# Making the low halves of weight tiles with ACT and an adding transfer instead of DVE, in a fused attention, feed-forward and retention kernel

## The chip, the cores and the metric

The kernel runs on one core of a Trainium2 chip. The metric is device time in microseconds for one launch. The engines are named as the profile names them: PE multiplies matrices, DVE and ACT work on vectors, POOL and SP mostly issue transfers here.

## What is computed

Two transformer-like blocks in a row, on 512 tokens with 1024 channels, in fp32. The first is differential attention beside a gated convolution, then a feed-forward part with a short convolution; the second is two layers of retention beside a short convolution. Cut to the products with weights, which is where the work is:

```python
# first_block (528 positions: 16 meta tokens + 512)
z = rms(h) @ w_in                       # 1024 -> 7168: q, k, v, glu, two gates
u = glu_a * sigmoid(glu_b);  u = causal_dwconv(u, 31 taps);  u = silu(layernorm(u))
y_conv = u @ w_conv_out
m = sigmoid(g_att) * y_att + sigmoid(g_conv) * y_conv
h = h + m @ w_out
up = causal_dwconv(rms(h) @ w_up, 3 taps)   # 1024 -> 5632
h = h + (silu(gate) * val) @ w_down         # 2816 -> 1024
# second_block, two layers
proj = rms(x) @ w_in[l]                 # 1024 -> 8192: c_b, c_c, c_x, c_z, r_q, r_k, r_v, r_z
x = x + rms(concat(conv part, retention part) @ w_out[l])
```

## The kernel before

**How a product is made exact enough.** PE multiplies in a rounded fp32 format (`float32r`). To keep fp32 accuracy, each weight tile and each activation tile is held as two halves: a high half (the value rounded) and a low half (the value minus its high half). A product is then three passes: high weight by high activation, low weight by high activation, high weight by low activation. In `proj` (line 150) these are the three entries of `passes`; each pass is 8 matmuls over the 1024 rows, so one weight tile of 128 by 1024 feeds 24 matmuls per chunk of tokens.

**How weights come.** The list `order` holds all 300 weight tiles (512 KB each, eight of them 384 KB) in the order in which PE will use them. `prep` (line 126) brings the next one: SP issues the transfer of the raw tile into `wraw`, ACT writes the high half `wh` as a rounding copy (line 138), DVE writes the low half `wl` as raw minus high (line 139). `wraw` has two buffers; `wh` and `wl` have four each. `getw` (line 142) hands out tiles and keeps four prepared or in preparation, so the halves of tile i go into the buffers that tile i-4 leaves when PE is done with it. PE is done with `wl` after its second pass, and with `wh` after its third.

**What sets the order.** Each engine executes its own queue strictly in order; waits are on semaphores. The order within a queue is made at build time by a list scheduler that plays the program through a timeline of its own, so a changed instruction also moves others.

**The stages, in order of time.** Gated linear unit (PE tiles `gv`, `gg`), attention heads (`v`, `q`, `k`, `ga`, `gc`, with scores `s`, transposes `tr`, outputs `po`, and per-head sums `pss`), beside them the 31-tap convolution on DVE (line 405), then `yc` and `wo`, feed-forward `up` and `dn`, and twice a retention stage (`rv`, `rq`, `rk`, `rz`, `st`, `ro`), a convolution stage (`cc`, `cx`, `cb`, `cz`) and an output stage (`w`). The queue of POOL carries, before the change, the moves `qh` and `kk` of attention (eight per head, lines 493 and 506), `hre` (line 642), `dc` of retention (line 838) and a few additions.

Of the kernel before, what the change touches and what calls it, by code (L numbers as in the profile page):

```python
# [13 lines left out]
AF = mybir.ActivationFunctionType  # L14
ALU = mybir.AluOpType
# [25 lines left out]
KB = 1  # L41
PSF = (4, 3, 1)
GC_EARLY = 5

PAR = {}
_off = 0
# [17 lines left out]
def kernel(ctx, tc, hT, par, pos, decay, w1, w2, out):  # L64
    nc = tc.nc
    V, S, PE = nc.vector, nc.scalar, nc.tensor
# [7 lines left out]
    def fv(ap):  # L74
        return ap.bitcast(F32)
# [4 lines left out]
    def w1_tiles(name, idx):  # L80
        order.append((w1[name], idx))
# [4 lines left out]
    for h in range(HEADS):  # L86
# [5 lines left out]
        if h < HEADS - 1:  # L92
            w1_tiles("w_in", 40 + h)
        if h < GC_EARLY:
            w1_tiles("w_in", 48 + h)
    w1_tiles("w_in", 40 + HEADS - 1)
    for n in range(GC_EARLY, NK):
        w1_tiles("w_in", 48 + n)
# [27 lines left out]
    def prep():  # L126
        if state["next"] >= len(order):
            return
        src, idx = order[state["next"]]
        i = state["next"]  # L130
        state["next"] += 1
        src = src[idx]
        n = src.shape[1]
        raw = wpool.tile([P, D], F32, tag="wraw", bufs=2, name=f"wraw{i}")[:, :n]
        nc.sync.dma_start(raw, src)
        wl = wpool.tile([P, D], F32R, tag="wl", name=f"wl{i}")
        wh = wpool.tile([P, D], F32R, tag="wh", name=f"wh{i}")
        S.copy(wh[:, :n], raw)  # L138
        V.tensor_tensor(wl[:, :n], raw, fv(wh[:, :n]), ALU.subtract)  # L139
        ready.append((wh, wl))  # L140

    def getw():
        while len(ready) < LOOK + 1 and state["next"] < len(order):
            prep()
        return ready.pop(0)
# [37 lines left out]
    def later(steps, by=20000):  # L183

        at_ = tc.cur_priority
        tc.cur_priority = at_ + by
        steps()
        tc.cur_priority = at_
# [75 lines left out]
    for c0, cn in C528:  # L264
        for j in range(NK // 2):
            nc.sync.dma_start(ht2[j][:, :, c0:c0 + cn], hT[2 * j:2 * j + 2, :, c0:c0 + cn].rearrange("k p t -> p k t"))
            if c0 == 0 and j in (0, 3):
                prep()
        if c0 == 0:
            nc.sync.dma_start(pr[:, 8:], par[:, 8:])  # L270
# [167 lines left out]
    def g_conv(n):  # L438
        w = getw()
        if n < 6:  # L440
            t = ap1.tile([P, TQ], F32, name=f"tgc{n}")
        else:
            t = upool.tile([P, CONV_K - 1 + T1], F32, tag="u", name=f"tgc{n}")
        for i, (c0, cn) in enumerate(C514):
            ps = mmA(f"gc{n}_{i}")[:, :cn]
            proj(ps, w, xh, xl, TQ0 + c0, cn)
            S.activation(t[:, c0:c0 + cn], ps, AF.Tanh, scale=0.5)
        tgc.append(t)

    def g_att(h):  # L450
        w = getw()
        tg = ap2.tile([P, TQ], F32, tag="tga", name=f"tga{h}")
        for i, (c0, cn) in enumerate(C514):
            ps = mmA(f"ga{h}_{i}")[:, :cn]
            proj(ps, w, xh, xl, TQ0 + c0, cn)
            S.activation(tg[:, c0:c0 + cn], ps, AF.Tanh, scale=0.5)
        return tg
# [8 lines left out]
    for h in range(HEADS):  # L466
# [41 lines left out]
        if h < HEADS - 1:  # L508
            tg = g_att(h)
        if h < GC_EARLY:  # L510
            g_conv(h)
        if h == HEADS - 1:
            att_rstd(("kf", "kl"))
            tg = g_att(h)
            later(norm_2, N2)
            for n in range(GC_EARLY, NK):
                later(lambda: g_conv(n), GCL)
# [11 lines left out]
        for t, (q0, qn, nkey) in enumerate(QT):  # L529
# [40 lines left out]
            src = ptr[:, :nb * qw].rearrange("p (b q) -> p b q", b=nb)  # L570
# [190 lines left out]
    for l in range(2):  # L761
# [38 lines left out]
        for h in range(HEADS):  # L800
# [66 lines left out]
            for j, i0 in enumerate((0, 128, 256, 384)):  # L867
                n = SEQ - i0
# [203 lines left out]
```

## Time and profile before

| what | value |
|---|---|
| time, median of 3 runs | 1881.17 us (1880.52 to 1882.43) |
| the profiled execution: its own time | 1883.03 us |
| the profiled execution: span from first to last instruction | 1881.2 us |
| PE busy | 1852.5 us, 98% |
| DVE busy | 1311.3 us, 70% |
| ACT busy | 836.1 us, 44% |
| POOL busy | 76.6 us, 4% |
| transfers | 177.79 MB, mean 95 GB/s |
| mean granted clock of PE | 0.995 |

The profiled execution took 1.9 us more than the median, and 1.83 us of its time lie outside the span. A busy share is an average over stages; which engine holds up a stage is read from the waits of PE in it. A transfer that is in flight is not counted as busy time of the engine that issued it.

### The profile page before, as it was taken

How to read it: one execution, taken by the hardware profiler on the slowest of the kernel's cores; microseconds unless marked ns; L12 is line 12 of the kernel's file. 1: busy time of each engine (PE TensorE's matmuls, PEld its weight loads, DVE VectorE, ACT ScalarE, POOL GpSimd, SP SyncE). 2: the span in 40 equal slices, each digit the busy share in tenths (PEclk: the TensorE clock that was granted, in tenths of full speed). 3: DMA queues.
4: the chain of work that ended last, by engine and by line, in shares of the span. 5: the costliest groups of instructions: out<-in, count | busy, mean ns of one | idle time of the engine just before them, and what ended most of it. 6: DMA issues, size and time to landing. Idle time of an engine off the chain costs nothing.

```text
span 1881.2 us, 29256 instructions
## 1 busy us (share of the span) xinstructions
PE 1852.5 (98%) x11802; PEld 1685.7 (90%) x11802; DVE 1311.3 (70%) x2147; ACT 836.1 (44%) x1473; POOL 76.6 (4%) x123
## 2 busy tenths in 40 slices
PE   8999999999999999999999999999999999999997
PEld 7999999988999999988988888888899888888887
DVE  8999999876688777634588776454277877745424
ACT  7234455673445444433356553222355555422222
POOL 3000011000000000000000000000020000000000
PEclk9999999999999999999999999999999999999999
DMA  4332323222332222232323222222213222222221
GB/s 153 101 113 91 102 87 118 89 70 68 113 107 91 96 96 91 85 104 93 99 75 107 79 91 90 100 101 91 100 68 101 95 92 93 79 101 92 99 101 56
DMA packets 53047, 177.79 MB, mean 95 GB/s; under 512 B 6640, under 2 KB 10736, under 8 KB 52912
## 3 DMA queue, kind: packets, MB, share of 16 engines
q1 hardware_dynamic: 47696, 160.80, 24.8%
q0 software_dynamic: 5072, 15.12, 2.9%
q8 instruction: 93, 1.52, 0.3%
q14 instruction: 42, 0.34, 0.1%
q10 hardware_dynamic: 144, 0.00, 0.0%
HBM read 165.25 MB, written 2.10 MB: 89 GB/s over the span
## 4 chain that ended last, share of the span: by engine, by line
PE 96%; ACT 2%; DVE 1%; DMA 0%; issue 0%; POOL 0%; SPq 0%; DVEq 0%; ACTq 0%
PE up L157 13%; PE w L157 9%; PE dn L157 6%; PE rz L157 5%; PE cb L157 5%; PE cc L157 5%; PE cx L157 5%; PE cz L157 5%; PE rv L812 5%; PE rq L157 5%; PE rk L157 5%; PE v L479 3%; PE gc L157 3%; PE yc L157 3%; PE wo L157 2%; PE q L157 2%
## 5 line engine op out<-in xcount | busy, mean ns | idle before, releaser
L138 ACT CAST wh<-wraw 128x1024 fp32r<-128x1024 f32 (+1 forms) x300 | 313.3, 1045 | 490.3 <-PE dn L157 66.8
L139 DVE TENSOR_TENSOR wl<-wraw,wh 128x1024 fp32r<-128x1024 f32 (+1 forms) x300 | 364.4, 1215 | 189.2 <-ACT wh L138 188.6
L157 PE MATMUL up<-xhome,wh 128*128 128x258 f32 x1408 | 183.7, 283 | 0.0
L157 PEld LDWEIGHTS up<-xhome,wh 128*128 128x128 f32 x1408 | 175.3, 190 | 0.1
L405 DVE SCALAR_TENSOR_TENSOR y<-u,pr,y 128x514 f32<-128x514 f32 x240 | 170.2, 743 | 0.3
L157 PE MATMUL up<-xhome,wl 128*128 128x258 f32 x704 | 97.9, 281 | 0.0
L157 PEld LDWEIGHTS up<-xhome,wl 128*128 128x128 f32 x704 | 89.7, 189 | 0.0
L725 DVE SCALAR_TENSOR_TENSOR cv<-cg,pr,cv 128x256 f32<-128x256 f32 x176 | 83.7, 479 | 7.9 <-ACT cv L722 6.5
L722 ACT ACTIVATE cv<-cg,pr 128x256 f32<-128x256 f32 x88 | 52.7, 599 | 63.3 <-DVE cg L719 63.3
L812 PE MATMUL rv<-wh,xhome 128*128 128x256 f32 x512 | 75.5, 286 | 0.0
L157 PE MATMUL rq<-xhome,wh 128*128 128x512 f32 (+1 forms) x288 | 70.1, 373 | 1.3 <-ACT xhome L238 1.3
L812 PEld LDWEIGHTS rv<-wh,xhome 128*128 128x128 f32 x512 | 67.9, 191 | 1.7 <-issue 0.5
L157 PE MATMUL rk<-xhome,wh 128*128 128x512 f32 (+1 forms) x288 | 68.5, 368 | 0.0
L157 PE MATMUL rz<-xhome,wh 128*128 128x512 f32 x256 | 65.9, 391 | 0.0
L157 PE MATMUL w<-mh,wh 128*128 128x512 f32 (+1 forms) x320 | 65.7, 348 | 0.0
L157 PE MATMUL w<-mh,wl 128*128 128x512 f32 (+1 forms) x320 | 65.4, 347 | 0.0
L157 PE MATMUL cx<-xhome,wh 128*128 128x512 f32 x256 | 64.0, 390 | 0.0
L157 PE MATMUL cc<-xhome,wh 128*128 128x512 f32 x256 | 63.7, 390 | 0.0
L157 PE MATMUL cb<-xhome,wh 128*128 128x512 f32 x256 | 63.7, 389 | 0.0
L895 DVE RECIPROCAL rsq<-rsq 128x512 f32<-128x512 f32 x16 | 53.6, 3350 | 14.0 <-ACT rsq L894 14.0
L157 PE MATMUL cz<-xhome,wh 128*128 128x512 f32 x256 | 63.3, 389 | 0.0
L157 PE MATMUL w<-ml,wh 128*128 128x512 f32 (+1 forms) x300 | 62.4, 348 | 0.0
(379 smaller groups left out, 4000.1 us busy)
## 6 DMA issues: line engine op xcount, KB each, us to landing
wraw<-w_in SPq DMA_DIRECT2D x160, 512.0 KB, 3.2
wraw<-w_up SPq DMA_DIRECT2D x44, 512.0 KB, 3.2
wraw<-w_out SPq DMA_DIRECT2D x40, 512.0 KB, 3.2
wraw<-w_v SPq DMA_DIRECT2D x24, 512.0 KB, 3.2
wraw<-w_down SPq DMA_DIRECT2D x16, 512.0 KB, 3.2
qh<-qf POOLq DMA_DIRECT2D x32, 129.0 KB, 2.7
wraw<-w_conv_out SPq DMA_DIRECT2D x8, 512.0 KB, 3.2
dc<-dec POOLq DMA_DIRECT2D x16, 256.0 KB, 3.1
```

Source lines behind the costliest of these rows:

```text
L138: S.copy(wh[:, :n], raw)
L139: V.tensor_tensor(wl[:, :n], raw, fv(wh[:, :n]), ALU.subtract)
L157: PE.matmul(ps, lhsT=a[:, ks(k)], rhs=b[k][:, t0:t0 + n], start=first and i == 0, stop=last and i == len(steps) - 1)
L405: V.scalar_tensor_tensor(ys[i][:, :TQ], src, wj, ys[i][:, :TQ], ALU.mult, ALU.add)
L479: PE.matmul(ps, lhsT=x, rhs=w, start=p == 0 and k == 0, stop=p == 2 and k == NK - 1)
L722: S.activation(t, g[:, 0:256], AF.Identity, scale=pr[:, o:o + 1], bias=pc("ffn_dw_b", f))
L725: V.scalar_tensor_tensor(t, g[:, k:k + 256], pr[:, o:o + 1], t, ALU.mult, ALU.add)
L812: PE.matmul(ps, lhsT=xx, rhs=w, start=p == 0 and k == 0, stop=p == 2 and k == NK - 1)
L895: V.reciprocal(rr, rr)
```

## The change

For tiles 6 to 299 the low half is no longer a subtraction on DVE. ACT writes the negative high half straight into `wl` (a copy with scale -1, rounded in the same way), and POOL then issues a transfer that reads the raw tile a second time from memory and adds it to what stands in `wl`. Tiles 0 to 5 are made as before. The high half and the transfer into `wraw` stay.

```diff
+ADDED = (6, 400)
...
         raw = wpool.tile([P, D], F32, tag="wraw", bufs=2, name=f"wraw{i}")[:, :n]
-        nc.sync.dma_start(raw, src)
         wl = wpool.tile([P, D], F32R, tag="wl", name=f"wl{i}")
         wh = wpool.tile([P, D], F32R, tag="wh", name=f"wh{i}")
-        S.copy(wh[:, :n], raw)
-        V.tensor_tensor(wl[:, :n], raw, fv(wh[:, :n]), ALU.subtract)
+        if ADDED[0] <= i < ADDED[1]:
+
+            nc.sync.dma_start(raw, src)
+            S.copy(wh[:, :n], raw)
+            S.activation(wl[:, :n], raw, AF.Copy, scale=-1.0)
+            nc.gpsimd.dma_start(wl[:, :n], src, accum_op=ALU.add)
+        else:
+            nc.sync.dma_start(raw, src)
+            S.copy(wh[:, :n], raw)
+            V.tensor_tensor(wl[:, :n], raw, fv(wh[:, :n]), ALU.subtract)
```

The build also moves instructions. On ACT, at the end of attention (head 7; `ssq` are the sums of squares of heads 4 to 7, `aTA` and `aTB` the transposed scores that PE needs next), this stood before:

```order
L589 COPY ssq_3191<-pss_194_4840 1x320
L222 ACT_TABLE_LOAD
L222 ACTIVATE ssq_3191<-ssq_3191,epsc 128x514
L138 CAST wh_5549<-wraw_5546 128x1024
L572 COPY aTA_5261<-tr_0_5281 128x66
L572 COPY aTA_5261<-tr_1_5302 128x2x128
L572 COPY aTB_5262<-tr_2_5324 128x3x128
L161 CAST rstd_kf<-ssq_3191 128x514
L572 COPY aTB_5262<-tr_3_5347 128x4x128
```

In the changed kernel the same stretch of ACT's queue reads:

```order
L597 COPY ssq_3224<-pss_194_4887 1x320
L142 ACTIVATE wl_5602<-wraw_5601 128x1024
L230 ACT_TABLE_LOAD
L230 ACTIVATE ssq_3224<-ssq_3224,epsc 128x514
L141 CAST wh_5603<-wraw_5601 128x1024
L580 COPY aTA_5314<-tr_0_5334 128x66
L580 COPY aTA_5314<-tr_1_5355 128x2x128
L169 CAST rstd_kf<-ssq_3224 128x514
L142 ACTIVATE wl_5671<-wraw_5670 128x1024
L141 CAST wh_5672<-wraw_5670 128x1024
L580 COPY aTB_5315<-tr_2_5377 128x3x128
```

One rounding copy stood between the sums and the last transposes; now two negative copies and two rounding copies stand there.

On ACT in the convolution stage of the second block (`yv`, `ct`, `mh` belong to one group of 128 channels) the queue was:

```order
L138 CAST wh_13531<-wraw_13528 128x1024
L937 ACTIVATE ct_13416<-ct_13416 128x512
L161 CAST mh_13521<-yv_13450 128x512
L138 CAST wh_13564<-wraw_13561 128x1024
L138 CAST wh_13600<-wraw_13597 128x1024
L927 ACTIVATE yv_13592<-pp_13525,pr 128x512
```

and is now:

```order
L141 CAST wh_13753<-wraw_13751 128x1024
L142 ACTIVATE wl_13789<-wraw_13788 128x1024
L141 CAST wh_13790<-wraw_13788 128x1024
L935 ACTIVATE yv_13783<-pp_13714,pr 128x512
L142 ACTIVATE wl_13823<-wraw_13822 128x1024
L141 CAST wh_13824<-wraw_13822 128x1024
```

Each rounding copy has got a negative copy of the same tile ahead of it.

On POOL, in the retention stage of the first layer, the moves `dc` (the decay table of one head, two buffers) stood one behind the other:

```order
L838 DMA dc_10753<-dec 128x512
L838 DMA dc_11099<-dec 128x512
L838 DMA dc_11316<-dec 128x512
L838 DMA dc_11614<-dec 128x512
L838 DMA dc_11818<-dec 128x512
```

Now the adding transfers stand between them:

```order
L143 DMA wl_11344<-w_in 128x1024
L846 DMA dc_11463<-dec 128x512
L143 DMA wl_11450<-w_in 128x1024
L846 DMA dc_11764<-dec 128x512
L143 DMA wl_11457<-w_in 128x1024
L143 DMA wl_11574<-w_in 128x1024
```

A `dc` whose buffer is not free now holds back the adding transfers behind it.

## Rows read from the trace of the kernel before

**Rows 1.** The page: busy time of the engines, share of the span, instructions.

```profile
span 1881.2 us, 29256 instructions
PE 1852.5 (98%) x11802; PEld 1685.7 (90%) x11802; DVE 1311.3 (70%) x2147; ACT 836.1 (44%) x1473; POOL 76.6 (4%) x123
```

**Rows 2.** Windows (start:end): length, busy us of each engine, PEclk, DMA share, GB/s.

```profile
0.00:20.00 20.00, 11.29 (x52) 9.98 (x53) 13.91 (x38) 15.26 (x34) 12.77 (x16) 1.00 0.65 227
20.00:300.00 280.00, 279.57 (x2305) 275.27 (x2305) 268.48 (x486) 126.25 (x277) 25.40 (x44) 1.00 0.31 101
300.00:487.00 187.00, 179.77 (x1382) 171.30 (x1381) 141.55 (x278) 107.24 (x238) 13.35 (x26) 0.98 0.26 83
...
1120.00:1297.00 177.00, 177.00 (x788) 146.76 (x787) 99.63 (x126) 54.28 (x67) 0.00 (x0) 1.00 0.27 95
1374.00:1417.00 43.00, 41.67 (x310) 39.74 (x309) 34.25 (x48) 23.85 (x54) 13.60 (x16) 0.96 0.26 86
...
1857.00:1881.20 24.20, 13.21 (x103) 12.35 (x101) 13.64 (x19) 3.00 (x8) 0.00 (x0) 0.82 0.26 87
```

**Rows 3.** Waits of PE: who waited for whom, us in total, times, longest.

```profile
PE gv L157 <- ACT wh L138: 8.2, 2, 6.2
PE tr L569 <- ACT aTA L572: 1.7, 2, 1.3
...
PE po L580 <- ACT ssq L589: 1.2, 2, 0.6
PE lnv L210 <- ACT rs_ln L222: 1.2, 1, 1.2
PE yc L157 <- DVE tgc L607: 1.2, 1, 1.2
PE k L157 <- DVE ql L490: 1.1, 2, 0.7
PE gc L157 <- ACT rs_ln L222: 0.6, 1, 0.6
PE tr L569 <- ACT aTB L572: 0.6, 1, 0.6
```

**Rows 4.** The page's groups: busy us, mean ns | idle before, releaser.

```profile
L138 ACT CAST wh<-wraw 128x1024 fp32r<-128x1024 f32 (+1 forms) x300 | 313.3, 1045 | 490.3 <-PE dn L157 66.8
L139 DVE TENSOR_TENSOR wl<-wraw,wh 128x1024 fp32r<-128x1024 f32 (+1 forms) x300 | 364.4, 1215 | 189.2 <-ACT wh L138 188.6
```

**Rows 5.** Timeline, convolution stage: start, us, engine line op [idle before].

```profile
1195.36 1.98 PE L157 MATMUL cx<-xhome,wl 128*128 128x512 f32 x8
...
1199.23 1.05 ACT L138 CAST wh<-wraw 128x1024 fp32r<-128x1024 f32 x1 [4.39 <-PE cx L157]
1200.19 0.72 ACT L927 ACTIVATE yv<-pp,pr 128x512 f32<-128x512 f32 x1
1200.31 1.23 DVE L139 TENSOR_TENSOR wl<-wraw,wh 128x1024 fp32r<-128x1024 f32 x1 [0.44 <-ACT wh L138]
...
1213.05 0.62 ACT L161 CAST mh<-yv 128x512 fp32r<-128x512 f32 x1 [1.36 <-DVE yv L938]
...
1217.12 1.98 PE L157 MATMUL cx<-xhome,wl 128*128 128x512 f32 x8
```

**Rows 6.** Transfers: queues (packets, MB, share of 16 engines), issues (us to landing).

```profile
q1 hardware_dynamic: 47696, 160.80, 24.8%
q0 software_dynamic: 5072, 15.12, 2.9%
...
wraw<-w_in SPq DMA_DIRECT2D x160, 512.0 KB, 3.2
...
dc<-dec POOLq DMA_DIRECT2D x16, 256.0 KB, 3.1
```

**Rows 7.** Groups of POOL: issuing of transfers, busy us, mean ns | idle before.

```profile
L493 POOL DMA_DIRECT2D qh<-qf x32 | 16.5, 526 | 320.4 <-ACT qf L488 136.6 <-issue 58.1 <-ACT p L563 32.9
...
L838 POOL DMA_DIRECT2D dc<-dec x16 | 8.8, 549 | 682.0 <-PE dn L157 376.7 <-DVE sd L873 305.3
```

**Rows 8.** Timeline of ACT at the end of attention.

```profile
435.68 0.42 ACT L589 COPY ssq<-pss 1x320 f32<-1x320 f32 x1 [1.64 <-PE pss L587]
436.12 1.28 ACT L222 ACT_TABLE_LOAD   x1
437.41 0.73 ACT L222 ACTIVATE ssq<-ssq,epsc 128x514 f32<-128x514 f32 x1
438.04 1.03 ACT L138 CAST wh<-wraw 128x1024 fp32r<-128x1024 f32 x1
439.10 0.21 ACT L572 COPY aTA<-tr 128x66 f32<-128x66 f32 x1
```

**Rows 9.** Waits of SP's queue (the raw tile's buffer).

```profile
SPq L135 <- DVE wl L139: 1371.0, 242, 23.1
```

## The prediction

> **What bounds the kernel now.** I read the busy times first: PE is busy 1852.5 of 1881.2 us, DVE 70%, ACT 44%, POOL 4% [rows 1]. So the whole idle time of PE is 1881.2 - 1852.5 = 28.7 us, and an edit that takes work off DVE can win part of that and no more. Next, the windows show where the idle time lies [rows 2]: 20 - 11.29 = 8.7 us in the first 20 us, 0.4 us from 20 to 300, 187 - 179.77 = 7.2 us from 300 to 487, 1.3 us from 1374 to 1417, and 24.2 - 13.21 = 11.0 us at the very end. That is 28.6 of the 28.7 us; everywhere else PE has no gap. Then the waits of PE tell who is waited for [rows 3]. Its largest wait, 8.2 us, is for the first high halves at the start. Within attention the waits are short: for ACT 1.7, 1.2, 1.2, 0.6 and 0.6 us, for DVE 1.2 (`tgc`) and 1.1 (`ql`). None is for a low half of a weight tile. So the start (tiles 0 to 5 are made as before) and the end (no weights left to prepare) are out of reach; what the change can touch is 7.2 + 1.3 + 0.4 = 8.9 us of idle time, 0.5% of the time.
>
> **What it removes.** 294 subtractions on DVE of 1215 ns [rows 4]: 294 x 1.215 = 357 us, so DVE falls to some 954 us. It is almost all beside PE's work. From 20 to 300 DVE is busy 268 of 280 us and PE still 279.57 [rows 2], so a full DVE costs PE next to nothing there. What may go are the two waits for DVE in attention, 1.2 + 1.1 = 2.3 us [rows 3]. The low half is also off the raw tile's release: SP's queue waited 1371 us in total for the subtraction [rows 9] and will wait for ACT's copies instead. That wait has cover, since no wait of PE after the first 20 us is for a high half or a raw tile [rows 3], so I count it at nothing; uncovered, it would show as PE waiting for `wh`.
>
> **What it adds on ACT.** 294 negative copies of 1024 columns. The trace has none, but brackets it: the rounding copy of the same tile takes 1045 ns [rows 4]; a scaled copy of 512 columns (`yv`) takes 0.72 us against 0.62 for a rounding copy of the same width (`mh`) [rows 5], a ratio of 1.16. So between 1.05 and 1.21 us. I take 1.05, the row with the same tile, and get 294 x 1.05 = 309 us, ACT at some 1145 us (61%); at 1.21 it is 356 us and 63%. In most stages this is free time: ACT works 54 of 177 us from 1120 to 1297 [rows 2]. It is not free where PE already waits for ACT. At the end of attention ACT's sums, table load, root and one rounding copy stand in a row from 435.68 to 439.07 ahead of the copies `aTA` that PE waits for [rows 8]. The new order puts one negative copy more ahead of `aTA`, and one more, with a rounding copy, ahead of `aTB`. I price that at two negative copies, 2 x 1.05 = 2.1 us. The bounds are 0, if PE's own fill-in work moves with it, and 7.4 us, worked out under the second rival.
>
> **What it adds on POOL.** 294 issues. An issue takes 526 to 549 ns for 64 or 128 rows [rows 7], so at least 294 x 0.549 = 161 us, POOL at 13%. If the issue of an adding transfer needs twice that, 1.1 us, POOL is at 21%. In either case it is one tile per about 6.3 us (1881 / 300), so the engine itself is no bound. `qh`, `kk`, `hre` and `dc` now share its queue with the tiles.
>
> **What it adds on the transfer engines.** 294 more readings of 512 KB, each also reading and writing `wl`. The trace has no adding transfer, so I bound it by what moving the bytes takes. From below, the same as a plain raw tile: 24.8% of the span for 300 tiles [rows 6], 0.248 x 1881 / 300 = 1.55 us of all 16 engines per tile. From above, a read from memory and a separate move within the chip, one after the other: a packet of the raw queue takes 0.248 x 1881 x 16 / 47696 = 156 ns for 4 KB, one of the software queue 0.029 x 1881 x 16 / 5072 = 172 ns for 2.98 KB, or 236 ns for 4 KB; 156 + 236 = 392 ns is 2.5 times a plain packet. So 1 to 2.5 times, unless the addition itself is slower than moving. I take 2 times, two reads for one write, nearer to the upper end because both reads go through the same engine. That is 294 x 3.1 = 911 us of transfer time, 48% of the span beside the present 28%, some 77% in all, below full.
>
> The Trainium skill, page "Collectives: The Full Stack", section "The bandwidth ceiling: the fold count and why AG ≠ RS ≠ AR", says that an adding transfer is slower because each piece needs two source reads on one ring, not because the addition costs cycles, and measures a ratio of 1.93. By it the term would be 294 x 1.55 x 1.93 = 880 us, an estimate from that page, and the time would be the same; no row here shows an adding transfer, so nothing in this trace agrees or disagrees.
>
> **Is the low half there in time?** In the convolution stage the tile whose buffers `cx` leaves is used again by the next `cx`. PE's second pass there runs from 1195.36 and frees `wl` at about 1197.3; the rounding copy comes at 1199.23 and the subtraction at 1200.31, done at 1201.54; PE needs that low half at 1217.12 [rows 5]. So 15.6 us are spare today. With the change: ACT 1.05 us, twice that if the rounding copy is served first, issue 0.55, and a landing. A plain transfer of POOL lands in 3.1 us, a raw tile in 3.2 [rows 6]; with 1.55 us more for a second read some 4.8. From 1199.23 that makes 1199.23 + 2.1 + 0.55 + 4.8 = 1206.7, still 10 us ahead. So the latency is covered, even at three times the landing. What it costs if that cover is gone is the whole excess, once per tile.
>
> **The sum.** Against the profiled execution, 1883.0 us: -2.3 (waits for DVE) + 2.1 (ACT in the tail of attention) + 0 (transfers covered) = 1882.8. The profiled execution lies 1.9 us above the median of the runs, so this stands for 1881 us. That is no change: about 0.2%, or 3.8 us, is what a measurement of this kernel can tell from none.
>
> **Rivals.**
>
> *DVE's relief reaches the middle.* Conversely to my pricing, ACT's waits may themselves be late because DVE fed ACT late (softmax and convolution alternate between the two). Then all 8.9 us that can be touched go: 1881 - 8.9 = 1872, or about half of them, 1876. For it: DVE is busy 141.55 of 187 us from 300 to 487, more than ACT with 107 [rows 2]. Against it: five of the seven waits in attention name ACT.
>
> *ACT becomes the late one in attention (slower).* From 300 to 487 there are about 187 / 6.3 = 30 tiles; moving them makes ACT 107 + 30 x 1.05 = 139 us and DVE 142 - 36 = 105, so they change places. If a negative copy stands ahead of every instruction of ACT that PE waits for, the seven waits on `aTA`, `ssq`, `rs_ln` and `aTB` (2 + 2 + 1 + 1 + 1 times [rows 3]) each grow by 1.05, 7.4 us: 1888. It decides if the copies fall inside those chains at more than the one place that I saw in the new order.
>
> *The adding transfer becomes the bound (slower).* Where a tile takes PE 24 matmuls of 512 columns, from one `cx` use to the next four tiles later 1217.12 - 1195.36 = 21.76 us [rows 5], the period is 5.44 us, and the raw tile takes a DMA share of 0.27 [rows 2], 1.47 us. So an adding transfer of more than (5.44 - 1.47) / 1.47 = 2.7 times a plain one fills the engines there. At 3 times, the 120 tiles of such stages (64 `cc` to `cz`, 32 `w`, 24 `dn`) cost 4 x 1.47 - 5.44 = 0.44 us each: 1881 + 53 = 1934. At 4 times every tile costs 7.35 us: 294 x 7.35 = 2161 us, and with the start some 2180. For it: nothing here shows the rate of the addition. Against it: the upper bound from moving the bytes is 2.5. The same rival covers an issue on POOL that takes above 5 us instead of 0.55.
>
> That the change does not do what it says is excluded: the new order has the negative copies and the adding transfers on their queues.
>
> **How the numbers follow.** Forecast, covered: 0.59, with a range of its own from 1875 to 1888 (0.16 faster than 1877.4, 0.33 within, 0.10 slower). Relief: 0.12, faster. ACT late: 0.14, slower. Transfer as the bound: 0.15, slower. So faster 0.28, same 0.33, slower 0.39; the likeliest case is the covered one at 1881. The lower end is 1873, all idle time that can be touched but a microsecond. Upward the range takes in ACT late and the transfer bound up to about 3 times, 1930; some 0.1 above that and a few hundredths below are left out.
>
> **What would show it.** Right: DVE near 954 us, ACT near 1145, POOL above 230; PE busy still near 1852; no wait of PE for a `wl`; the DMA share in the convolution stage near 0.8; the landing of the adding transfer around 5 us; the tail of attention with PE waiting 2 us more for `aTA` or `aTB`, and `tgc` and `ql` gone from PE's waits. Wrong: a landing above 15 us or a DMA share at 0.95 and more with PE waiting for `wl` in `cx` or `up` (the transfer bound); PE waiting for `wh` late (ACT held by its new copies); or an idle time of PE below 24 us (relief).

## The result, and the profile after

The changed kernel took 1902.65 us (median of 3 runs, 1901.41 to 1903.36) against 1881.17 before: a ratio of 1.0111, with a 95% interval from 1.0094 to 1.0128. It is 21 us slower where no change was forecast. The profiled execution has a span of 1899.6 us at a mean granted clock of 0.994.

The page of the changed kernel, span and busy times (columns as in [rows 1]):

```profile
span 1899.6 us, 29632 instructions
PE 1856.7 (98%) x11802; PEld 1686.6 (89%) x11802; DVE 987.3 (52%) x1853; ACT 1123.0 (59%) x1769; POOL 330.4 (17%) x417
```

The work moved as the change says: DVE's busy time falls by 324 us, ACT's rises by 287 and POOL's by 254. PE's idle time grows from 28.7 to 1899.6 - 1856.7 = 42.9 us, which is 14.2 of the 18.4 us by which the span grew. The other 4.2 us are PE's own busy time, with the same number of matmuls. The windows of the changed kernel show where (columns as in [rows 2]):

```profile
20.00:300.00 280.00, 273.28 (x2222) 268.29 (x2222) 241.91 (x473) 160.20 (x312) 59.32 (x85) 0.99 0.69 168
300.00:487.00 187.00, 177.85 (x1385) 169.89 (x1385) 95.76 (x215) 124.23 (x255) 31.70 (x46) 0.98 0.61 144
487.00:907.00 420.00, 419.96 (x3094) 401.65 (x3094) 208.40 (x475) 262.06 (x407) 70.35 (x84) 1.00 0.83 189
907.00:920.00 13.00, 12.12 (x102) 11.92 (x101) 1.58 (x4) 6.89 (x10) 2.85 (x4) 1.00 0.64 143
920.00:1135.00 215.00, 210.57 (x1180) 183.28 (x1179) 128.23 (x198) 142.66 (x207) 31.82 (x39) 1.00 0.70 168
1135.00:1310.00 175.00, 175.00 (x779) 145.11 (x778) 63.35 (x93) 86.58 (x97) 26.78 (x31) 1.00 0.80 188
```

Where the transfer engines are busiest, in the feed-forward part (0.83) and the convolution stage (0.80), PE has no gap. The gaps are new in attention (20 to 300: 6.7 us of idle time instead of 0.4) and in the first retention stage (907 to 1135: 5.3 us, where before there was none). From 300 to 487 they grow from 7.2 to 9.1 us, and from 1375 to 1620, around the second retention stage, from 1.3 to 4.0 us; the first 20 us have 2.0 us less. PE's waits in the changed kernel name what came late (who waited for whom, us in total, times, longest):

```profile
PE s L545 <- DMA kk<-kl: 6.3, 3, 5.2
...
PE s L545 <- issue: 5.6, 1, 5.6
PE rk L165 <- DMA wl<-w_in: 2.9, 2, 2.3
```

`tgc` and `ql` of [rows 3] are gone. In their place PE waits in attention, before the scores `s`, for `kk`, a move of 132 KB inside the chip that the change doesn't touch, and in retention for the low half `wl` itself (2.9 us before `rk`, 0.9 before `rv`). The third row, "issue", is a wait for which the profile names no releaser; below it turns out to be one for `kk` too. The queues (packets, MB, share of 16 engines) and issues (KB each, us to landing) of the changed kernel answer to [rows 6]:

```profile
q0 software_dynamic: 47408, 168.23, 49.7%
q1 hardware_dynamic: 47696, 160.80, 23.3%
...
wraw<-w_in SPq DMA_DIRECT2D x160, 512.0 KB, 5.5
wl<-w_in POOLq DMA_DIRECT2D x154, 512.0 KB, 5.4
...
kk<-kf POOLq DMA_DIRECT2D x16, 132.0 KB, 8.6
kk<-kl POOLq DMA_DIRECT2D x16, 132.0 KB, 8.4
```

In the kernel before, the two `kk` rows of the same view read:

```profile
kk<-kf POOLq DMA_DIRECT2D x16, 132.0 KB, 2.9
kk<-kl POOLq DMA_DIRECT2D x16, 132.0 KB, 3.1
```

A raw tile takes 5.5 us to land instead of 3.2, and `kk` takes almost three times as long. The wait of 5.2 us can be followed row by row. The timeline of POOL in the changed kernel (start, us, engine line op, [idle before <- releaser]) shows three adding transfers around the four `kk` moves:

```profile
134.43 0.94 POOL L143 DMA_DIRECT2D wl<-w_in  x1 [3.96 <-ACT kf L169]
136.68 0.87 POOL L143 DMA_DIRECT2D wl<-w_in  x1 [1.31 <-ACT kf L169]
137.24 1.40 POOL L514 DMA_DIRECT2D kk<-kf  x2
138.31 1.34 POOL L514 DMA_DIRECT2D kk<-kl  x2
140.01 0.93 POOL L143 DMA_DIRECT2D wl<-w_in  x1 [0.36 <-ACT tga L464]
```

The chain of waits then holds one piece of 11.90 us, from the issue of a `kk` move to its landing, and PE's timeline shows who pays:

```profile
138.82 11.90 DMA kk<-kl
```

```profile
150.18 0.30 PE L545 MATMUL s<-kk,qh 128*66 128x80 f32 x1 [5.25 <-DMA kk<-kl]
```

The wait named "issue" is the same thing 230 us later, in the seventh of the eight heads. Again the chain holds a long `kk` piece, and PE's first `s` follows right behind it:

```profile
368.22 10.45 DMA kk<-kf
```

```profile
380.03 0.30 PE L545 MATMUL s<-kk,qh 128*66 128x80 f32 x1 [5.65 <-issue]
```

Together these waits before `s` are 6.3 + 5.6 = 11.9 us. Short windows around the first of them (columns as in [rows 2]) show the transfer engines full and what follows the wait:

```profile
140.00:144.90 4.90, 4.90 (x42) 4.73 (x40) 4.90 (x8) 1.31 (x2) 0.93 (x1) 1.00 1.04 254
145.00:150.00 5.00, 0.00 (x0) 0.00 (x0) 2.76 (x5) 3.54 (x5) 0.87 (x1) 0.82 1.07 264
150.00:153.00 3.00, 2.77 (x15) 2.65 (x16) 1.17 (x3) 0.25 (x1) 0.00 (x0) 0.50 1.03 190
153.00:156.00 3.00, 3.00 (x19) 3.00 (x19) 3.00 (x8) 0.72 (x4) 0.00 (x0) 0.65 0.69 218
156.00:160.00 4.00, 4.00 (x35) 4.00 (x35) 2.48 (x7) 2.58 (x8) 0.01 (x1) 1.00 0.01 4
```

The transfer engines are full from 140 to 153 (records that overlap make the share more than 1) and empty from 156 on. PE stands idle for 5 us, its granted clock falls to 0.50, the lower of the two levels (1.2 GHz), and is full again from 156 on. In the kernel before, the transfer engines are busy for a fifth of that time, and PE has no gap:

```profile
140.00:150.00 10.00, 10.00 (x89) 10.00 (x89) 9.42 (x17) 3.33 (x8) 0.00 (x0) 1.00 0.21 68
```

The clock explains little of the growth of PE's busy time, though. PE was busy at the lower level for 4.8, 3.7 and 3.1 us here (stretches from 148.2, 376.9 and 1418.0), 11.6 us in all, and for 10.2 us in the kernel before (from 394.3, 442.1 and 1404.7, behind waits of 0.25 to 1.25 us). Of the 1.4 us between them about half, 0.7 us, is lost by the clock. Where the other 3.5 of the 4.2 us come from isn't settled.

In retention it is the same picture with another victim. Windows of the changed kernel from 930 on:

```profile
930.00:938.00 8.00, 8.00 (x64) 7.52 (x63) 4.93 (x5) 3.57 (x5) 0.96 (x2) 1.00 0.00 0
938.00:947.40 9.40, 9.40 (x61) 8.56 (x61) 3.67 (x7) 3.04 (x5) 0.78 (x1) 1.00 0.92 223
947.40:949.70 2.30, 2.30 (x12) 1.91 (x11) 0.00 (x0) 2.21 (x3) 0.00 (x0) 1.00 0.02 9
```

The engines do nothing for 8 us, are nearly full for 9.4, and nothing again. The timelines of POOL, SP, ACT and PE there, one row of each:

```profile
936.98 1.80 POOL L143 DMA_DIRECT2D wl<-w_in  x2 [15.72 <-ACT wl L142]
```

```profile
938.60 1.27 SPq L140 DMA_DIRECT2D wraw<-w_in  x2
```

```profile
947.49 1.05 ACT L141 CAST wh<-wraw 128x1024 fp32r<-128x1024 f32 x1 [5.76 <-DMA wraw<-w_in]
```

```profile
957.64 0.96 PE L165 MATMUL rk<-xhome,wl 128*128 128x512 f32 x3 [2.25 <-DMA wl<-w_in]
```

Two adding transfers and two raw tiles start together: POOL and SP issue them within three microseconds. At 3.0 and 1.5 us of all engines each (worked out below) they need 9 us, and the raw tile is there after 947.49 - 938.60 = 8.9. ACT then makes its two copies, POOL issues, and the low half lands too late for PE by 2.25 us.

### The profile page after: what moved, and what is told of

It reads as the page before. It is cut to its first block, busy times and chain, and to the rows that moved or that the text cites. A ratio compares the mean times of both kernels' runs of the same rounds, so it can differ in the third digit from the quotient of the medians.

```text
span 1899.6 us, 29632 instructions
## 1 busy us (share of the span) xinstructions
PE 1856.7 (98%) x11802; PEld 1686.6 (89%) x11802; DVE 987.3 (52%) x1853; ACT 1123.0 (59%) x1769; POOL 330.4 (17%) x417
## 3 DMA queue, kind: packets, MB, share of 16 engines
q0 software_dynamic: 47408, 168.23, 49.7%
q1 hardware_dynamic: 47696, 160.80, 23.3%
## 4 chain that ended last, share of the span: by engine, by line
PE 69%; issue 16%; DMA 5%; ACT 3%; POOL 3%; DVE 2%; POOLq 0%; DVEq 0%; ACTq 0%
PE up L165 13%; PE dn L165 6%; PE w L165 5%; PE rv L820 4%; PE rz L165 3%; PE v L487 3%; POOL wl L143 3%; PE wo L165 2%; PE q L165 2%; PE rk L165 2%; PE cb L165 2%; PE cc L165 2%; PE cz L165 2%; PE cx L165 2%; PE gg L165 2%
## 5 line engine op out<-in xcount | busy, mean ns | idle before, releaser
L142 ACT ACTIVATE wl<-wraw 128x1024 fp32r<-128x1024 f32 (+1 forms) x294 | 308.6, 1053 | 306.5 <-PE w L165 48.8
L141 ACT CAST wh<-wraw 128x1024 fp32r<-128x1024 f32 (+1 forms) x294 | 306.4, 1043 | 119.7 <-DMA wraw<-w_in 40.7
L143 POOL DMA_DIRECT2D wl<-w_in x154 | 133.7, 872 | 727.7 <-ACT wl L142 634.0
L214 DVE TENSOR_TENSOR acc_post<-acc_post,sq_post 128x256 f32<-128x256 f32 x24 | 9.3, 422 | 128.5 <-ACT sq_post L213 128.5
L143 POOL DMA_DIRECT2D wl<-w_up x44 | 38.4, 873 | 202.8 <-ACT wl L142 192.3
L143 POOL DMA_DIRECT2D wl<-w_out x40 | 34.6, 866 | 171.2 <-ACT wl L142 171.2
```

The costliest lines, as they stand in the source:

```text
L142: S.activation(wl[:, :n], raw, AF.Copy, scale=-1.0)
L143: nc.gpsimd.dma_start(wl[:, :n], src, accum_op=ALU.add)
L214: eng.tensor_tensor(a, a, sq[:, :cn], ALU.add)
```

## The experiments

The theories after the result were three; the letters are those of the expectations below. C: the adding transfers fill the transfer engines in bursts, and other transfers on PE's path come late. Q: they stand ahead of `kk` and `qh` in POOL's queue, which would be a matter of the order on one queue. A: ACT's new copies are late. All ratios below are to the kernel before, measured beside each group of versions (1880.8 to 1881.0 us), with 95% intervals.

### Is it POOL's queue?

`moves_act` lets ACT issue `qh` and `kk`, `moves_sp` lets SP do it:

```diff
-nc.gpsimd.dma_start(fv(qh[...]), ...)
-nc.gpsimd.dma_start(fv(kk[...]), ...)
+nc.scalar.dma_start(fv(qh[...]), ...)     # moves_sp: nc.sync
+nc.scalar.dma_start(fv(kk[...]), ...)
```

> The changed kernel with one thing different: the eight moves qh and kk of each attention head are issued by ACT on its own hardware queue, no longer by POOL behind the adding transfers. Theory Q (the moves stand behind adding transfers in one software queue): their landing falls from 10 to 12 us at worst to 3 to 5, the waits of PE for kk (11.7 us in two places) go, the granted clock from 110 to 200 and from 300 to 400 us returns to 1.00, and the time falls by 12 to 16 us, to 1887 to 1891. Theory C (16 transfer engines that are 73% busy slow every transfer, whatever its queue): the moves still land at 8 us and more, and the time stays within 4 us of 1902. Theory A (the negative copies make ACT late): ACT gets eight issues more per head, the time stays or grows.

> As the run before, with the moves on the queue of SP, in line with the raw tiles. Q: the waits for kk go as with ACT, but raw tiles now stand behind moves that wait for q and k, so 1887 to 1896. C: 1898 to 1906, as long a landing as on POOL. A: as C, since nothing on ACT changes.

Measured: 1912.4 us, 1.0178 [1.0147, 1.0208], and 1914.46 us, 1.0179 [1.0164, 1.0194]. Both are slower than the change itself and miss what Q and C expected. That `moves_act` grew would fit A, which `neg_only` below excludes. The issues of `moves_act`:

```profile
kk<-kf ACTq DMA_DIRECT2D x16, 132.0 KB, 6.7
kk<-kl ACTq DMA_DIRECT2D x16, 132.0 KB, 7.7
```

On a queue without a single adding transfer `kk` still lands in 6.7 and 7.7 us, on SP's in 6.1 and 7.2, and PE's waits before `s` for transfers or without a named releaser come to 13.2 us with ACT's queue (11.9 in the changed kernel). So POOL's order is not what makes `kk` late; it accounts for 0.7 to 2.5 us of the landing at most. The Trainium skill, page "DMA: Bandwidth & Descriptors", section "Issuing engines are not separate DMA queues", says that transfers issued by different engines run on the same 16 transfer engines and interleave there; these two runs agree. Why both came out 10 and 12 us worse than with POOL's queue isn't settled: their other waits are spread over many places, and the build also put PE's and ACT's instructions into another order.

### Which stage?

`skip_att` leaves tiles 16 to 55 (attention) on DVE, `skip_att_ret` those of retention too. `only_att` and `only_ret` apply the change to these tiles alone:

```diff
-        if ADDED[0] <= i < ADDED[1]:
+        if ADDED[0] <= i < ADDED[1] and not 16 <= i < 56:             # skip_att
+        if ADDED[0] <= i < ADDED[1] and not (16 <= i < 56
+                or 140 <= i < 172 or 220 <= i < 252):                 # skip_att_ret
+        if 16 <= i < 56:                                              # only_att
+        if 140 <= i < 172 or 220 <= i < 252:                          # only_ret
```

> Adding transfers for all tiles from the sixth on but the 40 of attention (16 to 55), whose low halves DVE makes as before. Q puts most of the loss into attention: 1902.65 - 16, about 1886, with the rest (about 5 us) in retention, where PE waited 3.7 us for low halves. C and A spread the loss over tiles: 40 of 294 tiles are 14% of 21.5 us, so 1898 to 1901.

> The other half of the split: adding transfers for the 40 tiles of attention alone. Q: 1881 + 14 to 17, about 1896, with the same two waits for kk. C and A: 1881 + 3, about 1884. If the two halves do not add up to the whole loss of 21.5 us, the parts act on each other.

> Adding transfers for all tiles from the sixth on but those of attention (16 to 55) and of both retention stages (140 to 171 and 220 to 251). If the 3.5 us that were left without attention come from the waits for low halves in retention, this is 1880 to 1882, the time of the kernel before; if they come from the convolution, feed-forward or output stages, it stays near 1884.

> Adding transfers for the 64 tiles of the two retention stages alone. The difference of the two versions without attention, with and without retention, is 10.5 us. If retention has that price by itself, 1890 to 1893, with PE waiting for low halves in rv, rk and rz. If the price needs the adding transfers of the stages before it (a backlog), 1881 to 1885.

| kernel | us | ratio | landing of `kk` (kf, kl), us |
|---|---|---|---|
| skip_att | 1884.49 | 1.0021 [1.0011, 1.0030] | 2.9, 3.7 |
| only_att | 1891.56 | 1.0058 [1.0043, 1.0073] | 8.3, 8.7 |
| skip_att_ret | 1873.99 | 0.9964 [0.9951, 0.9977] | 3.0, 3.9 |
| only_ret | 1892.83 | 1.0053 [1.0035, 1.0071] | 2.9, 3.2 |

With attention's tiles back on DVE `kk` lands as before, and 1902.65 - 1884.49 = 18 us come back (the runs of `skip_att` spread from 1881.4 to 1889.1). The change to those 40 tiles alone brings back the late `kk`, and the same stop of PE at the same place:

```profile
149.99 0.30 PE L545 MATMUL s<-kk,qh 128*66 128x80 f32 x1 [4.66 <-issue]
```

It costs 10.6 us alone; why 18 in company isn't settled. By the times alone this split looked like theory Q (1886 for `skip_att`) rather than C, whose expectation spread the loss over all tiles (1898 to 1901), and `only_att` lies between the two (1896 and 1884). What excludes Q is the pair of runs above; what was wrong in C's expectation is the even spread, since a late transfer costs only where PE has nothing else to do: in all eight heads of the changed kernel the first `s` starts within 1.2 us of the last landing of `kk`, and PE stands idle for more than 1 us in two of them. Retention costs 1884.49 - 1873.99 = 10.5 us as a difference and 12 alone, and `only_ret`, within its expected 1890 to 1893, shows whom PE waits for, low halves first:

```profile
PE rk L165 <- DMA wl<-w_in: 2.9, 3, 2.2
PE rv L820 <- DMA wl<-w_v: 2.8, 2, 1.5
PE rz L165 <- DVE rvl L247: 2.4, 1, 2.4
```

What is left in `skip_att_ret`, 190 of the 294 tiles, with all of the stages that load the transfer engines most, makes the kernel 7 us faster than before, faster than either of its expectations.

### Which part of the mechanism?

`neg_only` keeps ACT's negative copy and drops the transfer. `plain` keeps copy and transfer but doesn't add. `add_on_dve` has DVE subtract again, without the negative copy, and keeps the adding transfer behind it:

```diff
             S.activation(wl[:, :n], raw, AF.Copy, scale=-1.0)
-            nc.gpsimd.dma_start(wl[:, :n], src, accum_op=ALU.add)     # neg_only
+            nc.gpsimd.dma_start(wl[:, :n], src)                       # plain, instead
...
-            S.activation(wl[:, :n], raw, AF.Copy, scale=-1.0)
+            V.tensor_tensor(wl[:, :n], raw, fv(wh[:, :n]), ALU.subtract)   # add_on_dve
```

> ACT writes the negative high half, and nothing is added: the second reading of the weight is left out, so the low half is the negative high half. This is the change without its transfers: DVE relieved, ACT loaded. C and Q: 1876 to 1884, kk lands in 3 us. A: 1895 and more. If it is below 1877, the relief of DVE is worth something by itself.

> The transfer into wl stays on the same queue at the same place, but copies instead of adding (so the low half is the whole weight, which leaves out the subtraction). Theory C (every transfer shares the 16 engines packet by packet, and a packet of an adding transfer holds an engine for 327 ns against 160 for a plain one): the landing of kk falls from 8.5 to about 5 us, the two long waits of PE for kk shrink to half, and the time to 1888 to 1894. Theory Q (one queue, first in first out) gives about the same, since the transfers ahead of the moves get shorter too. Theory A (the negative copies on ACT): 1900 to 1904, as ACT has the same work.

> The other half: DVE subtracts as before the change, ACT has no negative copies, and the adding transfer comes behind the subtraction (so the low half holds the weight once too often). C and Q: the loss stays, 1897 to 1906, with kk landing in 8 us and more. A: 1881 to 1885.

| kernel | us | ratio | DVE, ACT busy us |
|---|---|---|---|
| neg_only | 1878.04 | 0.9984 [0.9974, 0.9993] | 986.1, 1127.7 |
| plain | 1878.47 | 0.9989 [0.9980, 0.9998] | 986.1, 1123.7 |
| add_on_dve | 1901.47 | 1.0113 [1.0096, 1.0129] | 1313.5, 840.2 |

ACT's copies and DVE's relief together cost nothing: the kernel is 2.8 us faster, as C and Q expected and against theory A. The adding transfer, with ACT as it was, brings a loss of the same size, but by other waits, since its low half now comes later still, behind DVE's subtraction. Its waits for low halves in retention are

```profile
PE rz L165 <- DMA wl<-w_in: 4.2, 3, 1.8
PE rq L165 <- DMA wl<-w_in: 3.0, 2, 2.5
```

and 2.7 us more in `rv`, while the stops before `s` have shrunk to 1.3 us, although `kk` lands in 6.2 and 6.3 us. So this run shows that adding transfers cost about 20 us without ACT's copies, not that `kk` alone makes the loss. And `plain`, with the same issues on the same queue reading the same bytes from memory, costs nothing either, against the 1888 to 1894 that I expected. It is the cleanest of the three: in its trace and in that of the changed kernel the instructions of every engine stand in the same order. The software queue of `plain` and its landings:

```profile
q0 software_dynamic: 47408, 168.23, 29.5%
...
wl<-w_in POOLq DMA_DIRECT2D x154, 512.0 KB, 3.6
...
kk<-kf POOLq DMA_DIRECT2D x16, 132.0 KB, 5.2
kk<-kl POOLq DMA_DIRECT2D x16, 132.0 KB, 5.6
```

Same packets, same bytes, 29.5% instead of 49.7%. At the place of the 5.25 us wait the engines of `plain` are nearly full too (0.90 from 140 to 150), but PE goes on without a gap; at the place of the 5.65 us wait it stops for 2.4:

```profile
140.00:150.00 10.00, 10.00 (x90) 10.00 (x89) 10.00 (x19) 5.56 (x12) 0.84 (x2) 1.00 0.90 275
```

So the adding itself makes the loss, not the queue, the number of issues or the bytes read from memory. With it each packet holds its engine longer, which is the account given here; POOL's longer issue comes with it too, some 0.34 us each by POOL's busy time (330 us against 231 in `plain`), and no run separates the two.

### A version that beats both

`glu_only` changes the tiles of the gated linear unit alone (6 to 15), `mid` those of the convolution's output and `wo` (56 to 71), `glu_mid` both:

```diff
-        if ADDED[0] <= i < ADDED[1]:
+        if 6 <= i < 16:                     # glu_only
+        if 56 <= i < 72:                    # mid
+        if 6 <= i < 16 or 56 <= i < 72:     # glu_mid
```

> Adding transfers for the ten tiles 6 to 15 of the gated linear unit alone. The version without attention and retention came out 6.9 us faster than before, and PE's waits in attention that it lost (5.9 us in the window from 385 to 470) hang on when the 31-tap convolution on DVE ends. If the gain comes from the early tiles (DVE gets ten subtractions, 12 us, ahead), this is 1874 to 1877. If it comes from the tiles near the end of attention, it stays at 1879 to 1882.

> Adding transfers for the 16 tiles of w_conv_out and w_out (56 to 71) alone, which are prepared while the last head ends. If the gain comes from DVE's chain at the end of attention, 1875 to 1878. If from the early tiles, 1880 to 1882.

> Tiles 6 to 15 and 56 to 71 together, 26 tiles. If feed-forward, convolution and output stages are indifferent, as PE never waits in them, this is the 1874 of the version without attention and retention, with a tenth of its adding transfers. If it is 1878 and more, something in the later stages gains as well.

| kernel | us | ratio |
|---|---|---|
| glu_only | 1871.66 | 0.9945 [0.9931, 0.9960] |
| mid | 1877.64 | 0.9981 [0.9971, 0.9990] |
| glu_mid | 1874.38 | 0.9957 [0.9942, 0.9972] |

Ten tiles give 9 us, the best time of all and better than the 1874 to 1877 that I expected for it; the sixteen of `mid` give 3 us by themselves, in the range expected for a gain from DVE's chain at the end of attention, and nothing on top. The page of `glu_only`, and its window over the end of attention (before: [rows 2], third row):

```profile
span 1869.2 us, 29285 instructions
PE 1846.2 (99%) x11802; PEld 1681.3 (90%) x11802; DVE 1301.1 (70%) x2137; ACT 848.5 (45%) x1485; POOL 84.3 (5%) x133
```

```profile
300.00:487.00 187.00, 185.06 (x1469) 178.69 (x1468) 138.35 (x275) 114.21 (x248) 13.89 (x27) 1.00 0.28 87
```

PE's idle time from 300 to 487 falls from 7.2 to 1.9 us and its granted clock rises from 0.98 to 1.00. The DVE line of the 31-tap convolution suggests why (durations, then first and last start), before and in `glu_only`:

```profile
L405 DVE SCALAR_TENSOR_TENSOR y<-u,pr,y x240: 631/745/755, 47.6 to 341.6; 128x514 f32<-128x514 f32 x120
```

```profile
L413 DVE SCALAR_TENSOR_TENSOR y<-u,pr,y x240: 631/748/765, 46.5 to 317.6; 128x514 f32<-128x514 f32 x120
```

Ten subtractions are 12 us of DVE, and the convolution, which DVE fills in beside attention, ends 24 us earlier. That this is what frees the end of attention is inferred from the two traces; no run delays the convolution by itself, and two others say that it isn't the whole of it. In `neg_only` the convolution's last start is at 269.0, earlier still, and PE has 5.5 us of idle time from 300 to 495; in `mid` it is at 341.4, as before, and there are 4.8 (7.2 before, 1.9 in `glu_only`). The order of the queues, which the build changes with every version, is a rival that isn't excluded.

## Why the prediction was wrong

**Bound, and what can be touched.** PE is the bound and stays it. The prediction took PE's idle time, 8.9 us of it [rows 2], as all that could be won, and left out that a wait can also lower the clock of the matmuls behind it. `glu_only` shortens the profiled span by 12 us (9.1 by the medians), 5.7 of idle time and 6.3 of PE's busy time. In it PE is busy at the lower clock for 3.4 us instead of 10.2, which at half speed is some 3.4 us of the 6.3; the other 2.9 aren't explained. The start wasn't out of reach either: it has 2.0 us less idle time in the changed kernel.

**What it removes.** DVE at 987 us against some 954. The busy times of DVE's groups sum to 1400.1 us before and 1043.6 after, so the 357 us did go; but neighbouring instructions overlap in the records, and the busy time of DVE as a whole falls by 324 only. The two waits for DVE, 2.3 us, went as priced. The cover of the raw tile's release held, as no wait for a high half came up beyond the start. "A full DVE costs PE next to nothing there" holds for PE's gaps from 20 to 300; downstream `glu_only` suggests that it costs something, by way of the convolution. The relief rival came nearest to this mechanism, with 1872 us, and `glu_only` measured 1871.66. That the numbers agree so well is luck: the rival took all 8.9 us of idle time to go, and 5.7 went.

**ACT.** 294 copies at 1.05 us: measured 1053 ns each, 308.6 us. In the tail of attention I priced 2.1 us. In `neg_only`, where nothing else is added, the wait on `aTA` is 2.9 us against 1.7 [rows 3], so 1.2, within the bounds; in the changed kernel it is 0.9, less than before, so there the term was nothing. The ACT rival (1888) falls with `neg_only`.

**POOL.** 0.549 to 1.1 us per issue; measured 860 to 873 ns. The queue's order, which I priced at nothing, isn't the cause.

**The size of the adding transfer.** I took 2 times a plain one, 3.1 us of all engines. Measured: (0.497 - 0.029) x 1899.6 / 294 = 3.02 us, against 0.233 x 1899.6 / 300 = 1.48 for a raw tile, 2.05 times. The ratio of 1.93 that the prediction cites from the Trainium skill's page "Collectives: The Full Stack", measured there between two collectives (AllGather and ReduceScatter), is close to it. The upper bound of 2.5 was worked out wrongly: a packet of the raw queue carries 160.80 MB / 47696 = 3.37 KB on average [rows 6], not 4, which makes it 2.2; the value taken, 2, isn't touched by that. The total, 73% against some 77%, stayed below full, and the transfer as a general bound (from 2.7 times on) did not come about: PE has no gap at 0.80 and 0.83. The measured time lies inside the range that I gave, but that is luck: the range reached so far up for this rival and for ACT coming late, and neither happened.

**The step that failed: "0 (transfers covered)".** The sum put the price of the new transfers at nothing. I checked the latency of the low half in the convolution stage alone, where it is right: PE has no gap there. I then let that stand for all stages, with a DMA share averaged over the span. Two things were left out. First, the adding transfers slow every other transfer on the same engines: I wrote that `qh`, `kk`, `hre` and `dc` share POOL's queue and never asked when PE needs `kk`. PE stopped twice for over 5 us, 11.9 us in all before `s`, at a DMA share of 1.04 to 1.07 around the first stop. Second, weights don't come evenly: in retention the share goes 0.00, 0.92, 0.02, and in the burst the raw tile takes 8.9 us instead of 3.2, so ACT starts late and the low half is too late. By the runs attention costs 10.6 us alone and retention 12, and the ten tiles of the gated linear unit give 9 back; these parts don't add up to the 21 us, and what they do to each other stays open. What would have shown the first was in the trace before: the last of a head's four `kk` moves landed only 1.4 to 6.2 us ahead of that head's first `s` there, in the seventh head 1.4 (363.7 and 365.1). Both rivals on the slower side looked at other places.

## What to carry to other kernels

When a change adds load to the transfer engines, list every transfer that an engine waits for soon after its issue, and ask of each what happens if it lands two or three times as late; the average DMA share doesn't tell. A share near 1 in the few microseconds around that issue is the warning, though not yet the loss: `plain` has 0.90 there and no gap. Check the latency in the stage with the least lead, not in the steadiest. And a change that helps in one stage and hurts in another is worth taking by the stage: here ten tiles of 294 gave the best of all versions that were run.

## What the runs showed of the hardware

- A transfer that adds holds its engine longer than a plain one with the same packets and the same counted bytes. The 294 tiles are 42336 packets (47408 - 5072 [rows 6]). From the shares of the software queue less its 2.9% before, one takes 0.336 us in the changed kernel ((0.497 x 1899.6 - 0.029 x 1881.2) x 16 / 42336) and 0.189 us in `plain`: 1.8 times.
- POOL is busy longer for issuing one: the group row of the changed kernel has 872 ns, against 526 to 549 for the moves [rows 7].

```profile
L143 POOL DMA_DIRECT2D wl<-w_in x154 | 133.7, 872 | 727.7 <-ACT wl L142 634.0
```

- A move within the chip takes longer beside plain traffic too: `kk` takes 2.9 us before, 5.2 in `plain` and 8.6 with adding (`kf` rows). It takes 4.5 in `neg_only`, where no transfer is added; that the raw tiles run at other times there is a guess.
- After a wait of 5 us PE ran at half clock (0.50 granted) for some 5 us more. Short waits have come ahead of it as well: in the kernel before, PE waited 0.56, 1.16 and 0.60 us between 388 and 394 and then ran at 0.50 from 394.3 to 397.7.
